# Scores behind the next pair's in-projection, and dense products beside the last gate table, in a trunk of token mixing and product-key experts

## The chip, the cores and the metric

The kernel runs on one core of a Trainium2 chip. The core's engines are TensorE (PE; its weight load is listed apart as PEld), VectorE (DVE), ScalarE (ACT), GpSimd (POOL) and SyncE (SP, which only issues transfers here). Each works off its own instructions in order, and waits where an operand is not there. What counts is the device time of one execution in microseconds (us), lower is better.

## The reference

One layer over 1024 rows (tokens) of 1024 columns, float32. A token mixer splits an in-projection into a gated convolution, a short convolution and a spatial gating, and projects back. Then comes the part that sets the time, a mixture of 16384 experts of one neuron each, 128 of which are picked for each token:

```python
q = (nf @ w_q).reshape(t, PEER_HEADS, D_KEY)                # 8 heads, two halves of 128
s1 = jnp.einsum("thd,hkd->thk", q1, sub_keys[:, 0])
s2 = jnp.einsum("thd,hkd->thk", q2, sub_keys[:, 1])
v1, i1 = lax.top_k(s1, TOPK)                                # 16 of 128 keys a half
v2, i2 = lax.top_k(s2, TOPK)
cand = (v1[..., :, None] + v2[..., None, :]).reshape(t, PEER_HEADS, TOPK * TOPK)
vals, ci = lax.top_k(cand, TOPK)                            # 16 of the 256 sums
idx = (e1 * N_KEYS + e2).reshape(t, PEER_HEADS * TOPK)
gates = jax.nn.softmax(vals, axis=-1)
# for each token t and each of its 128 picks k:
act = gelu(einsum("td,tkd->tk", xb, expert_u[idx])) * gates
out = einsum("tk,tkd->td", act, expert_v[idx])
```

A per-layer embedding with two projections and a final norm follow (the back).

## The kernel before

The rows are cut into eight tiles of 128. The kernel has three stages.

**Front.** Four pairs of tiles, (0,1), (2,3), (4,5), (6,7), go one after the other through `mix_in` (in-projection z, L158 and L207, in chunks through the PSUM tile `z`; convolution on VectorE, L179; norms; spatial gating, L232), `mix_out` (out-projection, L267, whose results are added to h, L269; normed h, L275, and its transposes) and `choose` (query product with w_q, L299; scores, L306; the top 16 of each half, L329 to L334; `select`, L338 to L394, which makes the keys, the gates and the indices). `mix_out` and `choose` call `fill()` sixteen times in a pair, and each call takes three steps from the list `filler`.

**Gate tables.** Four tiles (DENSE: 1 to 4) and one more (MIXED: 0) get a table of gates, expert block by token, built by `gate_table`. For four tokens at a time VectorE makes a one-hot of the first key (oh1, L415), and the one-hot of the second, times the gate, is made on POOL (L421) in every other group, else on ScalarE (L426, L427), or for MIXED on VectorE (L423). Four products (L430) put them together in a PSUM tile `gt`, ScalarE copies it to st (L431), and SyncE writes st to memory, Wd (L434). One product is recorded as two matmuls. The table of tile t is started once the tile's choose() is done; that of MIXED comes last, after its own activations are known: `u_step(MIXED, b, True)` gathers for it 128 rows of expert_u (POOL issues, L536; VectorE multiplies and sums up, L538, with three buffers `gathF`), and `u_step(GATHER[0], 0, True)` 32 more for tile 5.

**Dense and gathers.** For the four DENSE tiles all experts are computed. `u_stage(b)` does 24 matmuls for one block of 128 experts (L481 to L483, three for each of eight slices of columns, since a float32 factor is split into a high and a low part: uh by ScalarE, L468, ul by POOL, L470), then a gelu, the multiplication with the table w (L486) and the split into ah and al (L488, L490). `v_stage(g)` takes four blocks: ten products of twelve matmuls (L504 to L506) into the PSUM tile `mm` (two buffers), each of which VectorE adds to accA (L508). The fifth of the products' five tiles is MIXED, whose activations are its table itself (wm, split into mh and ml). `v` is split into vh and vl (L475 on ScalarE, L477 on POOL). Beside all this, `experts` gathers the experts of the three GATHER tiles (5 to 7): each of 128 gathers of u (L536, L538) and 128 of v (L566, L568) a tile is an issue on POOL and a product on VectorE, with five buffers.

**Back.** For each tile a norm, transposes (L594) and two projections (L612).

The order of the instructions on each engine isn't that of the text: the framework places them when the kernel is built, by its own simulated timeline, with the order of the text as priority, and the engines then keep that order. A pool of tiles that is laid where an earlier pool lay waits for the earlier pool's users; `fctx.close()` ends the pools of the front (work, gathF, group, wstream, rowp, wbp and the PSUM pool), and the pools of the dense stage come behind it.

## Time and profile before

| | us |
|---|---|
| median of three runs | 2855.62 |
| lowest and highest | 2852.89, 2864.11 |
| the profiled execution | 2862.61 |
| its span, first to last instruction | 2860.8 |
| TensorE busy | 2620.5 |
| VectorE busy | 2156.9 |
| POOL busy | 1945.5 |
| ScalarE busy | 1007.6 |

The profile is of one execution. A busy time is the time in which an engine worked on at least one instruction; what is left of the span is idle, and the trace names for each idle stretch the instruction whose end released it. "PEclk" is the clock that TensorE was granted, as a share of 2.4 GHz. In a window's row, the numbers behind the engines' busy times are counts of instructions.

### The profile page before, as it was taken

Reading aid. Unit: us, or ns where it says so; the run is one execution under the profiler, and the core shown is the slowest. Engines: PE = TensorE matmul, PEld = TensorE weight load, DVE = VectorE, ACT = ScalarE, POOL = GpSimd, SP = SyncE. Lnnn points to the kernel's source line nnn. Section 1 sums busy time; section 2 is a strip of 40 time slices with the busy share of each in tenths; the row PEclk is TensorE's granted clock in tenths of the full one; section 3 lists DMA queues with packets and bytes.
Section 4 is the critical chain, followed back from the end, with each engine's and each line's share of the span. In section 5 each row is a group of like instructions: output and inputs, shape, how many; then the busy total and the mean of one; then the engine's idle time right before and its main releaser. Section 6 shows DMA issues by size and latency. Waiting matters only on the chain.

```text
span 2860.8 us, 37645 instructions
## 1 busy us (share of the span) xinstructions
PE 2620.5 (92%) x12671; PEld 2203.2 (77%) x12671; DVE 2156.9 (75%) x4738; ACT 1007.6 (35%) x1930; POOL 1945.5 (68%) x1740
## 2 busy tenths in 40 slices
PE   7998999889678678999999999999999999999988
PEld 6887888688677656888787888878787788788767
DVE  5567888999977886777777777777777777677776
ACT  3312455335764544222322223232222322222342
POOL 0000377347876787888878888888887878888773
PEclk9998999899789779999999999999999999999999
DMA  6353688787657649899999999999999999999885
GB/s 203 129 185 120 236 300 301 242 304 253 221 206 274 228 184 339 317 324 344 331 333 328 331 347 330 338 329 342 325 336 329 328 348 332 335 339 324 299 290 174
DMA packets 299698, 820.92 MB, mean 287 GB/s; under 512 B 26096, under 2 KB 117616, under 8 KB 296944
## 3 DMA queue, kind: packets, MB, share of 16 engines
q0 software_dynamic: 129024, 469.82, 45.8%
q1 hardware_dynamic: 170480, 348.70, 35.6%
q8 instruction: 100, 1.64, 0.2%
q14 instruction: 94, 0.77, 0.1%
HBM read 764.93 MB, written 53.48 MB: 286 GB/s over the span
## 4 chain that ended last, share of the span: by engine, by line
PE 33%; DMA 23%; DVE 17%; POOL 13%; issue 10%; ACT 2%; SPq 0%; POOLq 0%; DVEq 0%; ACTq 0%
DMA g<-expert_u,idx 10%; DMA g<-expert_v,idx 10%; PE z L158 4%; DVE g L538 4%; POOL g L536 4%; PE mm L612 3%; POOL vl L477 3%; PE mm L504 3%; PE z L481 3%; PE z L482 3%; PE mm L505 3%; PE mm L506 3%; PE z L483 3%; PE mm L299 2%; PE mm L267 2%
## 5 line engine op out<-in xcount | busy, mean ns | idle before, releaser
L536 POOL DMA_INDIRECT g<-expert_u,idx x512 | 511.9, 1000 | 369.6 <-DVE g L538 163.2
L568 DVE SCALAR_TENSOR_TENSOR accP<-g,act,accP 128x1024 f32<-128x1024 f32 x384 | 493.2, 1284 | 210.9 <-DMA g<-expert_v,idx 207.4
L538 DVE SCALAR_TENSOR_TENSOR g<-g,nP 128x1024 f32<-128x1024 f32 x352 | 422.8, 1215 | 178.5 <-DMA g<-expert_u,idx 177.1
L566 POOL DMA_INDIRECT g<-expert_v,idx x384 | 367.7, 957 | 144.4 <-DVE accP L568 60.7
L504 PE MATMUL mm<-vh,ah 128*128 128x512 f32 x1024 | 400.3, 392 | 13.5 <-DVE accA L508 6.8
L481 PE MATMUL z<-nh,uh 128*128 128x512 f32 x1024 | 401.8, 393 | 8.1 <-DVE al L490 5.9
L482 PE MATMUL z<-nl,uh 128*128 128x512 f32 x1024 | 400.6, 391 | 2.0 <-DVE nl L446 2.0
L483 PE MATMUL z<-nh,ul 128*128 128x512 f32 x1024 | 400.2, 391 | 0.0
L505 PE MATMUL mm<-vl,ah 128*128 128x512 f32 x1024 | 399.2, 391 | 0.0
L506 PE MATMUL mm<-vh,al 128*128 128x512 f32 x1024 | 396.7, 390 | 0.0
L421 POOL TENSOR_SCALAR oh<-iota,eT,gT 128x128 f32<-128x128 f32 x320 | 314.5, 991 | 63.9 <-PE gt L430 50.8
L468 ACT CAST uh<-u 128x1024 fp32r<-128x1024 f32 x128 | 134.8, 1053 | 574.8 <-PE z L482 459.3
L477 POOL TENSOR_TENSOR vl<-v,vh 128x512 fp32r<-128x512 f32 x256 | 328.2, 1302 | 3.2 <-ACT vh L475 0.7
L470 POOL TENSOR_TENSOR ul<-u,uh 128x1024 fp32r<-128x1024 f32 x128 | 309.3, 2417 | 6.9 <-ACT uh L468 4.6
L430 PE MATMUL gt<-oh,oh 128*128 128x128 f32 x1280 | 221.4, 321 | 95.1 <-POOL oh L421 40.4
L430 PEld LDWEIGHTS gt<-oh,oh 128*128 128x128 f32 x1280 | 194.5, 224 | 123.1 <-POOL oh L421 82.6
L475 ACT CAST vh<-v 128x512 fp32r<-128x512 f32 x256 | 153.1, 621 | 306.9 <-DMA v<-expert_v 250.6
L538 DVE SCALAR_TENSOR_TENSOR g<-g,hrow 128x1024 f32<-128x1024 f32 x160 | 197.3, 1236 | 72.3 <-DMA g<-expert_u,idx 72.2
L158 PE MATMUL z<-aT,w 128*128 128x256 f32 x960 | 227.0, 393 | 16.0 <-DMA w<-w_inF 13.1
L299 PE MATMUL mm<-nT,w 128*128 128x256 f32 x1024 | 237.0, 383 | 4.4 <-DMA w<-w_q 4.4
L508 DVE TENSOR_TENSOR accA<-mm,accA 128x512 f32<-128x512 f32 x320 | 217.8, 684 | 27.0 <-PE mm L506 26.7
L504 PEld LDWEIGHTS mm<-vh,ah 128*128 128x128 f32 x1024 | 193.0, 189 | 56.7 <-DVE accA L508 9.8
(368 smaller groups left out, 4586.6 us busy)
## 6 DMA issues: line engine op xcount, KB each, us to landing
u<-expert_uT SPq DMA_DIRECT2D x128, 512.0 KB, 6.4
v<-expert_v SPq DMA_DIRECT2D x128, 512.0 KB, 4.9
Wd<-st SPq DMA_DIRECT2D x20, 2048.0 KB, 8.4
w<-w_q SPq DMA_DIRECT2D x64, 512.0 KB, 4.8
w<-Wd SPq DMA_DIRECT2D x128, 256.0 KB, 9.7
w<-w_inF SPq DMA_DIRECT2D x60, 512.0 KB, 3.6
wo<-w_out SPq DMA_DIRECT2D x32, 512.0 KB, 4.5
g<-expert_u,idx POOLq DMA_INDIRECT x512, 6.3
```

Source lines behind the costliest of these rows:

```text
L430: nc.tensor.matmul(pw[:, :, k], oh2[:, k], oh1[:, k], start=True, stop=True)
L477: nc.gpsimd.tensor_tensor(vl, v[:, s * 512:s * 512 + 512], vh.bitcast(F32), op=OP.subtract)
L481: nc.tensor.matmul(ph, uh[:, c], nh[:, c], start=c == 0, stop=False)
L482: nc.tensor.matmul(ph, uh[:, c], nl[:, c], start=False, stop=False)
L483: nc.tensor.matmul(ph, ul[:, c], nh[:, c], start=False, stop=c == 7)
L504: nc.tensor.matmul(po, ah[:, c], vh, start=i == 0, stop=False)
L505: nc.tensor.matmul(po, ah[:, c], vl, start=False, stop=False)
L506: nc.tensor.matmul(po, al[:, c], vh, start=False, stop=i == NG - 1)
L536: nc.gpsimd.indirect_dma_start(out=ug, out_offset=None, in_=expert_u, in_offset=bass.IndirectOffsetOnAxis(ap=idx[:, k:k + 1], axis=0))
L538: nc.vector.scalar_tensor_tensor(ug, ug, 1.0, ns[t, front], op0=OP.mult, op1=OP.mult, accum_out=dots[:, k - b * KB:k - b * KB + 1])
L566: nc.gpsimd.indirect_dma_start(out=vg, out_offset=None, in_=expert_v, in_offset=bass.IndirectOffsetOnAxis(ap=idx[:, kk:kk + 1], axis=0))
L568: nc.vector.scalar_tensor_tensor(acc, vg, act[:, k:k + 1], acc, op0=OP.mult, op1=OP.add)
```

## The change

Three things are changed.

The scores of a pair are computed one pair later. The loop now runs mix_in of a pair, then `finish` of the pair before (its choose, the list of tables to make, and for the last pair the gathers of MIXED), then mix_out of the pair. The last pair's `finish` stands behind the loop. (The branch `if t0 < 0` is never taken.)

Pools are laid out in another order. In the front, work and gathF stand behind group, wstream and rowp; wbp is allocated from the other side of the memory (`side="right"`); the tables' PSUM tiles (three of `gt`, and iotaP) have a pool of their own, psumT. Behind the front, psum2 is opened ahead of psumG, and hold and dm are allocated from the right.

The load of MIXED's wm and its split, and the loads of accA, stand in v_stage instead of u_stage and ahead of dense().

```diff
     fctx = ExitStack()
-    work = fctx.enter_context(tc.tile_pool(name="work", bufs=2))
-    gath = fctx.enter_context(tc.tile_pool(name="gathF", bufs=FG))
     group = fctx.enter_context(tc.tile_pool(name="group", bufs=1))
     wstream = fctx.enter_context(tc.tile_pool(name="wstream", bufs=2))
     rowp = fctx.enter_context(tc.tile_pool(name="rowp", bufs=2))
+    gath = fctx.enter_context(tc.tile_pool(name="gathF", bufs=FG))
+    work = fctx.enter_context(tc.tile_pool(name="work", bufs=2))
     fconst = fctx.enter_context(tc.tile_pool(name="fconst", bufs=1))
-    wbp = fctx.enter_context(tc.tile_pool(name="wbp", bufs=2))
+    wbp = fctx.enter_context(tc.tile_pool(name="wbp", bufs=2, side="right"))
     psum = fctx.enter_context(tc.tile_pool(name="psum", bufs=2, space=bass.MemoryType.PSUM))
+    psumT = fctx.enter_context(tc.tile_pool(name="psumT", bufs=3, space=bass.MemoryType.PSUM))
...
-    iotaP = psum.tile([P, P], F32, name="iotaP", bufs=1)
+    iotaP = psumT.tile([P, P], F32, name="iotaP", bufs=1)
...
-        pe = psum.tile([P, 4, P], F32, name="gt", bufs=3)
+        pe = psumT.tile([P, 4, P], F32, name="gt")
...
-                pw = psum.tile([P, P, 4], F32, name="gt", bufs=3)
+                pw = psumT.tile([P, P, 4], F32, name="gt")
...
                 ws[b // NG] = w
-                wm = dm.tile([P, P // TG, NG, TG], F32, name="wm")
-                nc.sync.dma_start(wm, Wd[MIXED][:, :, b:b + NG])
-                wm = wm.rearrange("p g n t -> p n g t")
-                mh = dm.tile([P, NG, P], F32R, name="mh")
-                mh_ = mh.rearrange("p n (g t) -> p n g t", t=TG)
-                nc.scalar.copy(mh_, wm)
-                ml = dm.tile([P, NG, P], F32R, name="ml")
-                nc.gpsimd.tensor_tensor(ml.rearrange("p n (g t) -> p n g t", t=TG), wm, mh_.bitcast(F32),
-                                        op=OP.subtract)
-                ms[b // NG] = mh, ml
...
         def v_stage(g):
+            b = g * NG
+            if g == 0:
+                for i, t in enumerate(TABLE):
+                    nc.sync.dma_start(accA[:, i], h1d[t])
+            wm = dm.tile([P, P // TG, NG, TG], F32, name="wm")
+            nc.sync.dma_start(wm, Wd[MIXED][:, :, b:b + NG])
+            wm = wm.rearrange("p g n t -> p n g t")
+            mh = dm.tile([P, NG, P], F32R, name="mh")
+            mh_ = mh.rearrange("p n (g t) -> p n g t", t=TG)
+            nc.scalar.copy(mh_, wm)
+            ml = dm.tile([P, NG, P], F32R, name="ml")
+            nc.gpsimd.tensor_tensor(ml.rearrange("p n (g t) -> p n g t", t=TG), wm, mh_.bitcast(F32),
+                                    op=OP.subtract)
+            ms[b // NG] = mh, ml
...
-    for t0, nt in ((0, 2), (2, 2), (4, 2), (6, 2)):
-        yT = mix_in(t0, nt)
-        choose(t0, nt, mix_out(t0, nt, yT))
+    def finish(t0, nt, nT):
+        choose(t0, nt, nT)
         if t0 == UAT:
             for b in range(P // KB):
                 u_step(MIXED, b, True)
         filler.extend(gate_table(t0 + t) for t in range(nt) if t0 + t in DENSE)
         if t0 == GAT:
             filler.append(gate_table(MIXED))
+
+    waits = []
+    for t0, nt in ((0, 2), (2, 2), (4, 2), (6, 2)):
+        yT = mix_in(t0, nt)
+        while waits:
+            finish(*waits.pop())
+        waits.append((t0, nt, mix_out(t0, nt, yT)))
+        if t0 < 0:
+            finish(*waits.pop())
+    finish(*waits.pop())
...
     fctx.close()
+    psum = ctx.enter_context(tc.tile_pool(name="psum2", bufs=2, space=bass.MemoryType.PSUM, reuse_waits="tile"))
     psumG = ctx.enter_context(tc.tile_pool(name="psumG", bufs=1, space=bass.MemoryType.PSUM, reuse_waits="tile"))
-    psum = ctx.enter_context(tc.tile_pool(name="psum2", bufs=2, space=bass.MemoryType.PSUM, reuse_waits="tile"))
-    hold = ctx.enter_context(tc.tile_pool(name="hold", bufs=1, reuse_waits="tile"))
+    hold = ctx.enter_context(tc.tile_pool(name="hold", bufs=1, side="right", reuse_waits="tile"))
     gath = ctx.enter_context(tc.tile_pool(name="gath", bufs=BG, reuse_waits="tile"))
     accA = hold.tile([P, NT, D], F32, name="accA")
-    for i, t in enumerate(TABLE):
-        nc.sync.dma_start(accA[:, i], h1d[t])
...
-    dm = dctx.enter_context(tc.tile_pool(name="dm", bufs=2, reuse_waits="tile"))
+    dm = dctx.enter_context(tc.tile_pool(name="dm", bufs=2, side="right", reuse_waits="tile"))
```

Where the instructions stand is seen by engine. In the changed kernel's rows, a line of the table's part is one higher than before (L431 for L430), and a line of u_stage nine lower (L472 for L481).

TensorE at the end of the MIXED table, before. L430 are table products of two groups (oh with their numbers), L481 to L483 those of u_stage:

```order
L430 MATMUL gt<-oh_8494,oh_8496 128x128
L430 MATMUL gt<-oh_8507,oh_8509 128x128
L430 MATMUL gt<-oh_8494,oh_8496 128x128
L430 MATMUL gt<-oh_8507,oh_8509 128x128 x3
L430 MATMUL gt<-oh_8494,oh_8496 128x128 x2
L481 MATMUL z<-nh,uh 128x512 x2
L482 MATMUL z<-nl,uh 128x512
L483 MATMUL z<-nh,ul 128x512
```

All 128 table products stand ahead of the first u-product. TensorE in the changed kernel, behind the first 58 table products:

```order
L431 MATMUL gt<-oh_8285,oh_8287 128x128
L472 MATMUL z<-nh,uh 128x512 x2
L431 MATMUL gt<-oh_8298,oh_8300 128x128
L431 MATMUL gt<-oh_8285,oh_8287 128x128
L431 MATMUL gt<-oh_8298,oh_8300 128x128 x3
L431 MATMUL gt<-oh_8285,oh_8287 128x128
L473 MATMUL z<-nl,uh 128x512
L474 MATMUL z<-nh,ul 128x512
```

The first u-products stand among the table's. TensorE in the changed kernel, at the end of the table, where L509 to L511 are the v-products:

```order
L431 MATMUL gt<-oh_8510,oh_8512 128x128
L472 MATMUL z<-nh,uh 128x512
L473 MATMUL z<-nl,uh 128x512
L474 MATMUL z<-nh,ul 128x512
L509 MATMUL mm<-vh,ah 128x512 x2
L510 MATMUL mm<-vl,ah 128x512
L511 MATMUL mm<-vh,al 128x512
```

165 u-products now stand ahead of the last table product, three more behind it, and then all 120 v-products of the first group in a row.

POOL at the end of the MIXED table, before. L421 are the table's one-hots, L536 gather issues of u, L470 ul, L462 ml, L477 vl:

```order
L421 TENSOR_SCALAR oh_8496<-iota,eT,gT 128x128 x4
L536 DMA g<-expert_u,idx 128x1024 x7
L470 TENSOR_TENSOR ul<-u,uh 128x1024
L536 DMA g<-expert_u,idx 128x1024
L470 TENSOR_TENSOR ul<-u,uh 128x1024
L462 TENSOR_TENSOR ml<-wm,mh 128x512
L477 TENSOR_TENSOR vl<-v,vh 128x512 x2
L536 DMA g<-expert_u,idx 128x1024
L477 TENSOR_TENSOR vl<-v,vh 128x512 x2
```

POOL there, in the changed kernel (L422, L541, L461, L496 and L468 are the same five):

```order
L461 TENSOR_TENSOR ul<-u,uh 128x1024
L422 TENSOR_SCALAR oh_8499<-iota,eT,gT 128x128 x4
L461 TENSOR_TENSOR ul<-u,uh 128x1024 x2
L541 DMA g<-expert_u,idx 128x1024 x7
L468 TENSOR_TENSOR vl<-v,vh 128x512 x4
L541 DMA g<-expert_u,idx 128x1024 x3
L496 TENSOR_TENSOR ml<-wm,mh 128x512 x2
L541 DMA g<-expert_u,idx 128x1024 x2
L468 TENSOR_TENSOR vl<-v,vh 128x512 x4
L541 DMA g<-expert_u,idx 128x1024 x5
```

Seven of the ul subtractions stand among the one-hots and two more ahead of the gather issues, and the fifteenth gather issue behind the table now stands behind two ml and eight vl. VectorE at the first addition into accA, before, where L538 are gather products, L486 the multiplication with the table, L490 the split and L508 the addition:

```order
L486 TENSOR_TENSOR z<-z,w 128x512
L538 SCALAR_TENSOR_TENSOR g,dots<-g,nP 128x1024
L490 TENSOR_TENSOR al<-z,ah 128x512
L486 TENSOR_TENSOR z<-z,w 128x512
L538 SCALAR_TENSOR_TENSOR g,dots<-g,nP 128x1024
L490 TENSOR_TENSOR al<-z,ah 128x512
L538 SCALAR_TENSOR_TENSOR g,dots<-g,nP 128x1024 x2
L486 TENSOR_TENSOR z<-z,w 128x512
L538 SCALAR_TENSOR_TENSOR g,dots<-g,nP 128x1024
L490 TENSOR_TENSOR al<-z,ah 128x512
L538 SCALAR_TENSOR_TENSOR g,dots<-g,nP 128x1024
L508 TENSOR_TENSOR accA<-mm,accA 128x512
```

VectorE there, in the changed kernel (L543, L477 and L513 are the gather product, the multiplication and the addition, L416 and L424 the table's one-hots):

```order
L416 TENSOR_TENSOR oh_8497<-iotaP,eT 128x512
L416 TENSOR_TENSOR oh_8510<-iotaP,eT 128x512
L424 TENSOR_SCALAR oh_8512<-iotaP,eT,gT 128x128 x4
L477 TENSOR_TENSOR z<-z,w 128x512 x2
L536 TENSOR_TENSOR nP<-nP,g_ffn 128x1024
L543 SCALAR_TENSOR_TENSOR g,dots<-g,nP 128x1024 x15
L513 TENSOR_TENSOR accA<-mm,accA 128x512 x2
L543 SCALAR_TENSOR_TENSOR g,dots<-g,nP 128x1024 x2
```

Before, 18 gather products stand ahead of the first addition, with multiplications and splits between them; now 15 stand in a row between the last multiplication of the table's time and the first addition.

## Rows read from the trace of the kernel before

**Rows 1.** The page's head, parts 1 and 2: busy time of the engines, granted clock by slice.

```profile
PE 2620.5 (92%) x12671; PEld 2203.2 (77%) x12671; DVE 2156.9 (75%) x4738; ACT 1007.6 (35%) x1930; POOL 1945.5 (68%) x1740
...
PEclk9998999899789779999999999999999999999999
```

**Rows 2.** Windows, all engines; columns as in their first line.

```profile
core 0: us, PE busy (x) PEld busy (x) DVE busy (x) ACT busy (x) POOL busy (x), PEclk, DMA share, GB/s
...
290.00:773.00 483.00, 418.53 (x2471) 371.60 (x2470) 436.53 (x1447) 228.72 (x523) 284.07 (x262) 0.93 0.76 267
773.00:1018.40 245.40, 190.47 (x1096) 172.47 (x1095) 196.89 (x753) 151.75 (x364) 178.51 (x173) 0.81 0.62 222
1018.40:1055.00 36.60, 23.64 (x113) 20.14 (x112) 27.44 (x73) 11.66 (x19) 28.94 (x34) 0.73 0.64 247
1055.00:1084.40 29.40, 23.24 (x147) 18.80 (x146) 22.88 (x54) 10.51 (x19) 27.50 (x36) 0.97 0.57 221
1084.40:1130.00 45.60, 34.91 (x128) 26.98 (x129) 30.21 (x49) 22.10 (x34) 31.36 (x25) 0.85 0.97 351
1130.00:1250.00 120.00, 120.00 (x530) 99.09 (x529) 84.83 (x108) 33.61 (x52) 97.07 (x82) 1.00 0.93 329
```

**Rows 3.** VectorE's waits from 290 to 1018 us: total, times, longest.

```profile
DVE g L538 <- DMA g<-expert_u,idx: 72.2, 39, 5.6
```

**Rows 4.** Window around the start of pair 1's out-projection; columns as in rows 2.

```profile
257.00:290.00 33.00, 20.98 (x93) 14.65 (x93) 29.87 (x182) 17.46 (x36) 0.56 (x1) 0.72 0.24 79
```

**Rows 5.** The page, parts 5 and 6: count, busy us, mean ns; us to landing.

```profile
L477 POOL TENSOR_TENSOR vl<-v,vh 128x512 fp32r<-128x512 f32 x256 | 328.2, 1302 | 3.2 <-ACT vh L475 0.7
L470 POOL TENSOR_TENSOR ul<-u,uh 128x1024 fp32r<-128x1024 f32 x128 | 309.3, 2417 | 6.9 <-ACT uh L468 4.6
...
L538 DVE SCALAR_TENSOR_TENSOR g<-g,hrow 128x1024 f32<-128x1024 f32 x160 | 197.3, 1236 | 72.3 <-DMA g<-expert_u,idx 72.2
...
g<-expert_u,idx POOLq DMA_INDIRECT x512, 6.3
```

**Rows 6.** TensorE's timeline around 782 us: start, length, line, count.

```profile
781.94 1.95 PE L430 MATMUL gt<-oh,oh 128*128 128x128 f32 x16
783.73 0.94 PE L267 MATMUL mm<-wo,yT 128*128 128x128 f32 x7
```

**Rows 7.** TensorE's timeline, end of the MIXED table and start of the dense stage.

```profile
1079.11 2.04 PE L430 MATMUL gt<-oh,oh 128*128 128x128 f32 x14 [0.28 <-DVE oh L423]
1081.48 0.49 PE L430 MATMUL gt<-oh,oh 128*128 128x128 f32 x2 [0.33 <-POOL oh L421]
1082.34 1.95 PE L430 MATMUL gt<-oh,oh 128*128 128x128 f32 x14 [0.37 <-DVE oh L423]
1086.52 0.73 PE L481 MATMUL z<-nh,uh 128*128 128x512 f32 x2 [2.23 <-ACT nh L445]
...
1088.86 0.63 PE L481 MATMUL z<-nh,uh 128*128 128x512 f32 x1
1089.29 0.63 PE L482 MATMUL z<-nl,uh 128*128 128x512 f32 x1
...
1109.63 1.22 PE L504 MATMUL mm<-vh,ah 128*128 128x512 f32 x2 [6.55 <-ACT vh L475]
```

**Rows 8.** POOL's timeline, the same stretch.

```profile
1058.37 25.38 POOL L421 TENSOR_SCALAR oh<-iota,eT,gT 128x128 f32<-128x128 f32 x32 [0.75 <-PE gt L430]
...
1091.13 0.94 POOL L536 DMA_INDIRECT g<-expert_u,idx  x1 [0.30 <-issue]
1092.37 0.94 POOL L536 DMA_INDIRECT g<-expert_u,idx  x1 [0.30 <-issue]
...
1109.75 1.29 POOL L462 TENSOR_TENSOR ml<-wm,mh 128x512 fp32r<-128x512 f32 x1
```

**Rows 9.** VectorE's timeline, its first addition into accA.

```profile
1139.00 0.69 DVE L508 TENSOR_TENSOR accA<-mm,accA 128x512 f32<-128x512 f32 x1 [3.07 <-PE mm L506]
```

**Rows 10.** Timelines of VectorE and TensorE: last gather product, last tile's transposes.

```profile
2828.86 1.28 DVE L568 SCALAR_TENSOR_TENSOR accP<-g,act,accP 128x1024 f32<-128x1024 f32 x1
...
2836.08 1.03 PE L594 MATMUL z<-ident,a 128*128 128x128 f32 x8
```

## The prediction

> **What bounds the kernel now.** I read the page's head first: TensorE is busy for 2620.5 us of the span, 92% [rows 1], so on average little is left to win, and the line of granted clocks falls under nine tenths only within the first 15 of the 40 slices. Then I cut the span by stage. The reader is to compare the busy time of each engine with the length of its stretch [rows 2]. From 1130 us on TensorE is busy throughout (120.00 of 120) at the full clock. Before that three stretches differ. From 290 to 1018.4 us, the front with the last three pairs, VectorE is busy for 436.53 of 483.00 and 196.89 of 245.40 us, 95 us short of all, and the list of its waits puts 72.2 us of those on gathers that had not landed [rows 3]. So the front is nearer to a VectorE bound than to a TensorE bound (418.53 and 190.47). From 1018.4 to 1084.4 us the mixed tile's table is made, and TensorE idles for 13.0 and 6.2 us. From 1084.4 to 1130 us the dense stage starts, and TensorE idles for another 10.7 us.
>
> The start of the dense stage can be given as a line. 128 matmuls were recorded up to 1130 us and 530 more in the next 120 us, one each 0.2264 us. Carried back, 658 x 0.2264 = 149 us before 1250, so at full pace the stage would have begun at 1101.0 us: 46.0 us behind 1055 us, the time by which 58 of the table's 128 products are done. I call 1055 us the midpoint, since the changed order puts the first dense product behind the same 58. Everything after is a line of dense products, so what the change is worth in the middle is how far this line moves, measured from the midpoint.
>
> **Part 1: choose() behind the next pair's in-projection.** No work is added or removed. Where a pair's out-projection starts, TensorE waits for the convolution's end on VectorE and ScalarE: around pair 1 it is busy for 20.98 of 33 us, at a clock of 0.72 [rows 4], and there are three such places. They are what deferring the scores fills. But VectorE is busy for 29.87 of those 33 us, and in the new order its own work is the same; filling TensorE there moves its work forward, and VectorE, which also has the top-16 searches and 160 gather products to do, ends when it ended. The gathers start later too, since the mixed tile's indices come out of the first choose(): 37 instead of 62 gather products stand ahead of the third pair's residual adds, 102 instead of 119 ahead of the fourth's, 158 instead of 160 ahead of the mixed table's first one-hot. The lead that TensorE gains is therefore paid back by the table. Bounds: at best VectorE loses every idle time but the gather waits, 95 - 72.2 = 23 us; at worst the 25 gather products that fall behind come out serial, at 1.24 us each [rows 5] 31 us later. I take -1, nearest to the counts at the table, which are within 2 of each other.
>
> **Part 2: dense products beside the mixed table.** The pools and banks are laid out anew so that the dense stage's buffers don't wait for the front's. In the order, the first u-product stands behind 58 table products, and 165 u-products stand before the last table product. TensorE's part of the second half: 70 table products at 0.224 us (16 records, two to a product, between the starts at 781.94 and 783.73 [rows 6]) are 15.7 us, and 165 x 0.2264 = 37.4 us, together 53 us. The table alone took 29.4 us there, paced by the one-hots on POOL and VectorE, 3.2 us to 8 products (16 records between the starts at 1079.11 and 1082.34 [rows 7]). POOL now also has 7 ul passes to do in it: 28.5 us for 36 one-hots at 0.79 (25.38 us for 32 [rows 8]) and 7 x 2.417 [rows 5] are 45 us, so TensorE stays the longest. I allow up to 9 us for in-order waits or for 48 products at the lower clock, where two products start 0.43 us apart rather than 0.2264 [rows 7]: 53 to 62, of which I take 55.
>
> What comes next is the part that I count against the change. Before, the dense products began 2.23 us behind the table [rows 7], the first v-product at 1109.63, and VectorE's first add into accA at 1139.00, behind 18 gather products that stood between small pieces of dense work [rows 9]. Now VectorE has 15 gather products in a row ahead of that first add, and no piece of dense work in between; the two PSUM buffers of the v-products fill with 24 matmuls, and the next one waits for the add. The 15 products wait for POOL, which has between the last one-hot and the 15th gather: 2 ul (4.8 us), 15 issues at the pitch of 1.24 us (18.6), 8 vl at 1.302 (10.4) and 2 ml at 1.29 (2.6), in all 36.4 us, from the starts 1091.13 and 1092.37 and the means [rows 5, 8]. Then the gather lands (6.3 us), is multiplied (1.2) and the add ends (0.7): 44.6 us behind POOL's last one-hot. POOL may be up to 5 us ahead of TensorE, so the third v-product starts 40 to 45 us behind the last table product. By then TensorE has done 165 + 3 u-products and 24 v-products, 192, worth 43.5 us of the line.
>
> Line after, from the midpoint: 53 + 40 - 43.5 = 49.5 at the least, 62 + 45 - 43.5 = 63.5 at the most, 55 + 44 - 43.5 = 55.5 taken. Before it was 46.0. So the dense stage is +3.5 to +17.5 us, I take +10. The table overlaps indeed, but the products that were put forward are the ones that waited for nothing before, and the first accumulation still waits for gathers that couldn't be issued during the table.
>
> **Part 3: wm and accA loaded in v_stage.** Per group of four expert blocks one SyncE load, one ScalarE cast and one POOL subtraction move from the u-stage to before the v-products, and the five loads of accA move into the first group; on SyncE they then stand behind the first loads of v. The count is the same, and the adds into accA wait for the gathers anyway. Nothing, as long as that 40 us wait is there; gone, it would cost one load ahead of the first add, for which the nearest row is a gather's 6.3 us [rows 5].
>
> **Tail.** 51 instead of 46 gathers are left after the last add into accA. The last gather product ends at 2828.86 + 1.28 and TensorE is busy with the back until 2836.08, when the last tile's transposes start [rows 10]: about 6 us of slack. Five gathers at 1.24 us each are 6.2 us, at 8.8 us for a ring of five (issue, landing, product) 8.8 us: 0 to +3, I take +1.5.
>
> **Sum.** -1 + 10 + 0 + 1.5 = +10.5 us. The profiled execution took 2862.61 us, 1.75 us over its span and 0.24% above the median of the runs, 2855.62; it becomes 2873, and the median 2866, +0.37%.
>
> **The rivals.** *Lockstep, slower.* In-order engines may not overlap the two streams at all. VectorE's w-multiplies stand between one-hots, so that a late u-product holds the table's next one-hot, and a late one-hot holds the u-products queued behind its table product. Then the second half is the sum of both, 29.4 + 37.4 = 66.8, and with gaps that hold the clock down for 48 products of the 165, 9.6 more: 76. The line moves to 76 + 43 - 43.5 = 75.5, +29.5, 2885 or 2886 with the tail. For it: TensorE's rows in the table are runs of 14 and 2 with a wait for an engine ahead of each [rows 7]. Against it: POOL and VectorE have room. It decides from a second half above 61 us, where the sum passes 0.5%.
>
> *The front gains, faster.* If the three bubbles at the out-projections are closed and VectorE's idle time that is not a gather wait goes with them, the front is 23 us shorter, and without the middle's loss 2833; with a part of it about 2840. For it: the low clock of 0.72 there, that the added work would lift. Against it: VectorE at 90%.
>
> *It does what it says, faster.* The table costs nothing, since dense products fill TensorE's idle time in all three stretches, 13.0 + 6.2 + 10.7 = 29.9 us, and the gathers land in time: 2826. For it: the idle time is there. Against it: the 15 gather products in a row. The Trainium skill, page "Perfetto Trace Analysis", section "Optimization Strategy", says that a kernel with several regimes may gain from interleaving them; by that rule, this is the result. The trace agrees in so far as the table and the dense stage have different busiest engines; no run here shows the two interleaved.
>
> **How the numbers follow.** The forecast has 0.45 with a range of its own of 2857 to 2879; lockstep 0.28; the front 0.15; the full overlap 0.12. About 0.5%, 14.3 us, is what a measurement of this kernel can tell from no change. The forecast's range passes 2870 with a ninth of its chance, 0.05. So: slower 0.28 + 0.05 = 0.33, the same 0.40, faster 0.15 + 0.12 = 0.27. The range for 8 in 10 runs from 2831, just below the front's case, to 2890, above lockstep; the full overlap and a still worse table are left out.
>
> **What would show it.** In the profile after: the table's last product 53 to 62 us behind its 59th; one TensorE wait of some 25 us or more for accA's add before the third v-product, with VectorE waiting for gathers from expert_u; a line 50 to 63 us from the midpoint; the midpoint itself within some 5 us of 1055. A midpoint earlier by 15 us or more shows the front's case; a TensorE without that one wait shows the full overlap; a second half above 66 us lockstep. I am wrong if the gathers are issued early enough, by a POOL that runs ahead of the table, to land before the table ends.

## The result, and the profile after

The changed kernel is slower. Its median is 2879.85 us, that of the kernel before, run beside it, 2855.95 us (11 runs each); the ratio is 1.0078, with a 95% interval of 1.0061 to 1.0096, so the change costs about 22 us, more than the 0.5% that can be told from none. The forecast was 2866 us, +10.5 us, which is within that 0.5%.

The traces show a part of this. The profiled execution took 2875.26 us (span 2873.5), 12.7 us more than that of before; a second pair of executions, e9 and e10 below, differs by 13.0 us. The two of before lie 6.7 and 11.8 us above the median of before, those of after 4.6 us below and 0.9 us above theirs. So the traces can account for about 13 us of the 22, and where the other 9 are is in no trace.

The page's head of the kernel after, parts 1 and 2, against [rows 1]:

```profile
PE 2606.5 (91%) x12671; PEld 2192.3 (76%) x12671; DVE 2160.6 (75%) x4738; ACT 1005.7 (35%) x1930; POOL 1962.5 (68%) x1740
...
PEclk9999999899889677999999999999999999999999
DMA  6354587777657667999999999999999999999885
```

TensorE and ScalarE work a little less than before, VectorE 3.7 and POOL 17.0 us more, and both of these have idle time left. The windows of after, with the columns of [rows 2]:

```profile
1018.40:1055.00 36.60, 23.63 (x118) 19.71 (x118) 35.03 (x88) 18.03 (x28) 32.27 (x28) 0.76 0.64 207
1055.00:1084.40 29.40, 26.58 (x151) 23.04 (x151) 18.55 (x39) 12.08 (x20) 24.84 (x24) 1.00 0.29 110
1084.40:1130.00 45.60, 27.09 (x145) 22.60 (x145) 23.41 (x44) 15.55 (x24) 27.72 (x26) 0.83 0.78 282
1130.00:1250.00 120.00, 104.98 (x441) 84.95 (x440) 79.84 (x108) 28.88 (x46) 94.46 (x83) 0.89 0.95 336
```

From 1055 to 1084.4 us TensorE is now busy for 26.58 of 29.40 us, against 23.24. In the next two stretches it gives this back: 27.09 instead of 34.91 of 45.6, and 104.98 instead of 120.00 of 120. The next column to look at is the last but one, the share of time in which the DMA engines moved something: 0.29 and 0.78, where it was 0.57 and 0.97.

The milestones, each worked out from the trace of one execution (us from the span's start; the midpoint is the start of the 59th of the mixed table's 128 products; the line is worked out as in the prediction, at 0.2267 us a product, from the count up to 1250 and up to 2640 us):

| | before | before again | after | after again |
|---|---|---|---|---|
| last score product | 964.1 | 971.4 | 946.0 | 949.2 |
| midpoint | 1056.8 | 1065.4 | 1052.2 | 1054.5 |
| the mixed table's last product ends | 1084.3 | 1092.9 | 1109.0 | 1111.3 |
| line of dense products, to 1250 | 1101.3 | 1109.7 | 1111.5 | 1114.0 |
| line of dense products, to 2640 | 1142.0 | 1148.3 | 1149.0 | 1153.5 |
| last add into accA starts | 2727.5 | 2730.9 | 2729.2 | 2734.9 |
| last gather product starts | 2828.9 | 2834.1 | 2841.1 | 2846.6 |
| span | 2860.8 | 2866.0 | 2873.5 | 2879.0 |

The second half of the table takes 56.8 us in both executions instead of 27.5. The delay of the dense products shrinks on the way: 10.2 and 4.3 us in the line up to 1250 us, 1.7 and 4.0 us at the last add into accA. The last gather product is 12.3 and 12.5 us later, nearly as much as the span. TensorE's timeline at its start and its end, of after:

```profile
1051.03 0.49 PE L431 MATMUL gt<-oh,oh 128*128 128x128 f32 x2 [0.73 <-POOL oh L422]
1051.27 0.73 PE L472 MATMUL z<-nh,uh 128*128 128x512 f32 x2
1051.87 1.58 PE L431 MATMUL gt<-oh,oh 128*128 128x128 f32 x12
...
1107.28 1.72 PE L431 MATMUL gt<-oh,oh 128*128 128x128 f32 x14
1122.76 1.22 PE L509 MATMUL mm<-vh,ah 128*128 128x512 f32 x2 [13.06 <-ACT vh L466]
1129.42 0.80 PE L510 MATMUL mm<-vl,ah 128*128 128x512 f32 x1 [5.45 <-POOL vl L468]
...
1147.45 1.22 PE L509 MATMUL mm<-vh,ah 128*128 128x512 f32 x2 [13.39 <-ACT vh L466]
```

u-products (L472) and table products (L431) do run side by side. Then TensorE waits three times, for 13.06, 5.45 and 13.39 us, and each time for the split of v. The wait that the prediction had named, for VectorE's first add into accA, isn't there. VectorE's timeline, first of before, then of after, shows its first gather product for the gather tiles and (after) its first add:

```profile
1088.31 1.21 DVE L538 SCALAR_TENSOR_TENSOR g<-g,nP 128x1024 f32<-128x1024 f32 x1
```

```profile
1113.65 1.22 DVE L543 SCALAR_TENSOR_TENSOR g<-g,nP 128x1024 f32<-128x1024 f32 x1
...
1154.17 1.49 DVE L513 TENSOR_TENSOR accA<-mm,accA 128x512 f32<-128x512 f32 x2 [9.26 <-POOL vl L468]
```

The add comes 45 us behind the table's last product, as forecast (44.6), but VectorE stood idle ahead of it for 9.26 us: it waited for TensorE's product (the row names vl, an operand of that product), and not TensorE for it. The first gather product stands 4.7 us behind the end of the table, much as before (4.0); it is 25.3 us later because the table ends 24.7 us later. Where the v's are late is seen on SyncE's queue and on ScalarE, of after:

```profile
1109.91 0.33 SPq L435 DMA_DIRECT2D Wd<-st  x1
...
1114.04 1.68 SPq L463 DMA_DIRECT2D v<-expert_v  x2
1117.41 2.24 SPq L488 DMA_DIRECT2D accA<-h1d  x5
1119.95 4.16 SPq L490 DMA_DIRECT2D wm<-Wd  x2
1124.69 8.79 SPq L533 DMA_DIRECT2D hrow<-h1d  x1
1133.58 2.85 SPq L463 DMA_DIRECT2D v<-expert_v  x2
```

```profile
1122.09 1.14 ACT L466 CAST vh<-v 128x512 fp32r<-128x512 f32 x2 [2.34 <-DMA v<-expert_v]
...
1143.42 0.62 ACT L494 CAST mh<-wm 128x512 fp32r<-128x512 f32 x1 [17.64 <-DMA wm<-Wd]
...
1146.78 1.14 ACT L466 CAST vh<-v 128x512 fp32r<-128x512 f32 x2 [1.94 <-DMA v<-expert_v]
```

The first two v's are asked for only behind the last write of the table, the next two 19.5 us later. POOL gives the first buffer back at 1130.60 us, and SyncE is held by the issue of hrow until 1133.48 us. Between the two pairs stand the five loads of accA and two of wm, whose cast holds ScalarE for 17.64 us. But the next vh, behind that cast, waits another 1.94 us for its own v, which lands 13.2 us after it was asked for. So what comes last is v and not the cast. The transfers issued from 1085 to 1165 us, with KB and median us to landing:

```profile
v<-expert_v SPq DMA_DIRECT2D x7, 512.0 KB, 8.0
...
accA<-h1d SPq DMA_DIRECT2D x5, 512.0 KB, 14.2
...
wm<-Wd SPq DMA_DIRECT2D x4, 256.0 KB, 12.8
```

Before, the first two v's also left 8 us behind the table's last write, and the next two 20 us later (1084.94, 1093.04 and 1113.54 us on SyncE). But then TensorE had all its u-products of the first group still to do, which covered them.

The end of the trace, ScalarE before, then ScalarE and TensorE after, against [rows 10]:

```profile
2833.31 1.15 ACT L588 ACTIVATE a<-hrow,r 128x1024 f32<-128x1024 f32 x1 [0.94 <-POOL r L122]
```

```profile
2846.05 1.13 ACT L593 ACTIVATE a<-hrow,r 128x1024 f32<-128x1024 f32 x1
2847.24 1.09 PE L599 MATMUL z<-ident,a 128*128 128x128 f32 x8 [3.80 <-ACT a L593]
```

Before, TensorE was through with the tile ahead at 2836.2 us and found the last tile's normed rows ready since 2834.5. After, it comes at 2843.4, 7.2 us later, and then waits another 3.80 us for them, since the last gather product is 12.3 us later. With 1.5 us of half-clock products behind this wait (30 products in 8.60 instead of 7.11 us) that is 12.5 of the 12.7 us. So in these traces it is the gathers that carry the loss to the end.

### The profile page after: what moved, and what is told of

Its sections match the earlier page's. It is cut to its first block, busy times and chain, and to the rows that moved or that the text cites. A ratio compares the mean times of both kernels' runs of the same rounds, so it can differ in the third digit from the quotient of the medians.

```text
span 2873.5 us, 37623 instructions
## 1 busy us (share of the span) xinstructions
PE 2606.5 (91%) x12671; PEld 2192.3 (76%) x12671; DVE 2160.6 (75%) x4738; ACT 1005.7 (35%) x1930; POOL 1962.5 (68%) x1740
## 3 DMA queue, kind: packets, MB, share of 16 engines
q0 software_dynamic: 129024, 469.82, 45.6%
## 4 chain that ended last, share of the span: by engine, by line
PE 40%; DMA 19%; DVE 19%; POOL 12%; issue 9%; ACT 1%; SPq 0%; POOLq 0%; DVEq 0%; ACTq 0%
DMA g<-expert_u,idx 9%; DMA g<-expert_v,idx 7%; DVE g L543 5%; PE mm L509 5%; PE z L472 4%; PE mm L510 4%; PE mm L511 4%; PE z L473 4%; PE z L474 4%; PE z L159 4%; PE mm L617 3%; POOL oh L422 3%; POOL g L541 3%; POOL vl L468 3%; PE mm L300 2%
## 5 line engine op out<-in xcount | busy, mean ns | idle before, releaser
L541 POOL DMA_INDIRECT g<-expert_u,idx x512 | 512.7, 1001 | 307.3 <-DVE g L543 130.3
L543 DVE SCALAR_TENSOR_TENSOR g<-g,nP 128x1024 f32<-128x1024 f32 x352 | 424.0, 1216 | 222.4 <-DMA g<-expert_u,idx 220.1
L509 PE MATMUL mm<-vh,ah 128*128 128x512 f32 x1024 | 403.3, 395 | 35.7 <-ACT vh L466 26.5
L472 PE MATMUL z<-nh,uh 128*128 128x512 f32 x1024 | 401.1, 392 | 9.6 <-DVE al L481 9.6
L511 PE MATMUL mm<-vh,al 128*128 128x512 f32 x1024 | 399.2, 393 | 1.0 <-DVE al L481 1.0
L422 POOL TENSOR_SCALAR oh<-iota,eT,gT 128x128 f32<-128x128 f32 x320 | 330.3, 1041 | 45.9 <-PE gt L431 40.9
L431 PE MATMUL gt<-oh,oh 128*128 128x128 f32 x1280 | 222.5, 321 | 127.8 <-DVE oh L416 66.6
L468 POOL TENSOR_TENSOR vl<-v,vh 128x512 fp32r<-128x512 f32 x256 | 328.1, 1301 | 3.4 <-ACT vh L466 0.9
L431 PEld LDWEIGHTS gt<-oh,oh 128*128 128x128 f32 x1280 | 198.2, 226 | 154.8 <-POOL oh L422 96.5
L461 POOL TENSOR_TENSOR ul<-u,uh 128x1024 fp32r<-128x1024 f32 x128 | 309.8, 2421 | 8.1 <-ACT uh L459 6.1
L543 DVE SCALAR_TENSOR_TENSOR g<-g,hrow 128x1024 f32<-128x1024 f32 x160 | 196.4, 1229 | 81.7 <-DMA g<-expert_u,idx 81.6
L509 PEld LDWEIGHTS mm<-vh,ah 128*128 128x128 f32 x1024 | 194.2, 190 | 82.0 <-ACT vh L466 27.6
L513 DVE TENSOR_TENSOR accA<-mm,accA 128x512 f32<-128x512 f32 x320 | 218.2, 684 | 30.7 <-PE mm L511 21.1
```

Source lines behind the costliest of these rows:

```text
L422: nc.gpsimd.tensor_scalar(oh2[:, k], iota, k2, gk, op0=OP.is_equal, op1=OP.mult)
L431: nc.tensor.matmul(pw[:, :, k], oh2[:, k], oh1[:, k], start=True, stop=True)
L468: nc.gpsimd.tensor_tensor(vl, v[:, s * 512:s * 512 + 512], vh.bitcast(F32), op=OP.subtract)
L472: nc.tensor.matmul(ph, uh[:, c], nh[:, c], start=c == 0, stop=False)
L509: nc.tensor.matmul(po, ah[:, c], vh, start=i == 0, stop=False)
L511: nc.tensor.matmul(po, al[:, c], vh, start=False, stop=i == NG - 1)
```

## The experiments

Where nothing else is said, ratios are to runs of the kernel before on the same chip.

### Part 1 alone, and parts 2 and 3 alone

The kernel before with the new loop (e1):

```diff
+    def finish(t0, nt, nT):
+        choose(t0, nt, nT)
...
     for t0, nt in ((0, 2), (2, 2), (4, 2), (6, 2)):
         yT = mix_in(t0, nt)
-        choose(t0, nt, mix_out(t0, nt, yT))
+        while waits:
+            finish(*waits.pop())
+        waits.append((t0, nt, mix_out(t0, nt, yT)))
+    finish(*waits.pop())
```

> The kernel before with part 1 alone: the scores of a pair behind the next pair's in-projection, pools and banks as before. The line from which the dense products run at full pace stood at 1101.3 us before and at 1111.5 us in the changed kernel. If the loss lies at the start of the dense stage (both theories below), the dense products start behind the table as before, the line stays within 4 us of 1101 and the time within 0.3% of the kernel before. If the delayed scores cost by themselves (fewer gathers done in the front, more of them left over behind the dense stage), the time is 0.4 to 0.8% above the kernel before with the dense line unmoved.

The kernel after with the old order of the scores (e2):

```diff
-        if t0 < 0:
+        if t0 >= 0:
             finish(*waits.pop())
-    finish(*waits.pop())
```

> The changed kernel with part 1 undone: each pair's scores follow its out-projection at once; pools, banks and the loads in v_stage as changed. If the loss lies at the start of the dense stage, it stays: 0.4 to 0.9% above the kernel before, with TensorE waiting for 25 us or more in pieces behind the table. If it is the delayed scores that cost, the time comes back to within 0.3% of the kernel before.

Measured: e1 2856.27 us, 0.9996 (0.998 to 1.0011); e2 2867.65 us, 1.0029 (1.0013 to 1.0044). e1's time is that of the kernel before, but its line isn't within 4 us of 1101: it stands at 1091.5, with the midpoint 18.5 us earlier than in before, in an execution that is the shortest of its twelve. e2's 0.29% is under the 0.4 to 0.9% of the one case and just inside the 0.3% of the other. The two parts together cost 0.78%, so parts 2 and 3 cost more where the scores are late. Why is not shown; in e2 the first u-product stands behind 17 of the 128 table products instead of 58, so that more of the table is there to be covered. TensorE's waits for v are there in e2 as well, from 1085 to 1200 us two for vh of 20.1 us in sum.

### A third buffer for v

```diff
-            v = dv.tile([P, D], F32, name="v")
+            v = dv.tile([P, D], F32, name="v", bufs=3)
```

> The changed kernel with three buffers for v instead of two, nothing else. Theory A (15 gather products of VectorE ahead of the first addition into accA hold the third v-product): 12 instead of 15 stand ahead of it now, so the line from which the dense products run at full pace moves from 1111.5 by 4 to 7 us at most, and TensorE's wait before the third block stays on the addition. Theory B (the loads behind the table come late: v of the third block waits for a buffer that POOL frees only behind seven gather issues, and TensorE waited 13.4 us for its cast): that wait falls under 6 us, and the line moves by 7 to 13 us, to 1099 to 1105; the time falls by 0.2 to 0.5% against the changed kernel.

Measured: 2884.44 us, 1.0082 (1.0061 to 1.0104). The line of products starts 0.9 us behind the table's last product instead of 2.5, and the two waits for vh are 26.7 us in sum, as in after (26.5). The third v is now loaded with the first two and its cast starts at 1121.43 us, so the second wait has moved from the third block to the fourth, whose v leaves at 1129.39 us only. Its buffer was free at 1124.29 us, but SyncE was held by the issue of hrow until 1129.29 us. A missing buffer alone isn't what makes the later v's late.

### Without the loads of accA

The kernel after; the five tiles' residual h is left out of the result, since the first group of products is copied into accA instead of added to what was loaded:

```diff
-            if g == 0:
-                for i, t in enumerate(TABLE):
-                    nc.sync.dma_start(accA[:, i], h1d[t])
...
-                nc.vector.tensor_add(o_, po, o_)
+                if g == 0:
+                    nc.vector.tensor_copy(o_, po)
+                else:
+                    nc.vector.tensor_add(o_, po, o_)
```

> The changed kernel without the five loads of accA (2.5 MB) behind the table; the first group's additions are copies, so the residual h1 of the five tiles is left out of what is computed. Theory A: 14 instead of 15 gather products ahead of the first write of accA, the line moves by 1 to 2 us. Theory B, with the traffic of the loads as its cause: 2.5 MB at the 400 GB/s of that stretch are 6 us, by which wm and v land earlier, and the line moves by 4 to 8 us.

Measured: 2870.99 us, 1.0049 (1.0032 to 1.0066). TensorE's timeline at the same two v-products:

```profile
1116.27 1.22 PE L506 MATMUL mm<-vh,ah 128*128 128x512 f32 x2 [13.34 <-ACT vh L466]
...
1130.68 1.22 PE L506 MATMUL mm<-vh,ah 128*128 128x512 f32 x2 [3.77 <-ACT vh L466]
```

The first wait stays, the second falls from 13.39 to 3.77 us, and the line starts 5.0 us ahead of the table's last product instead of 2.5 behind it: 7.5 us. SyncE's issue of hrow takes 0.33 instead of 8.79 us, and the next v leaves at 1123.48 us, as soon as POOL has freed its buffer. The ratios differ by 0.29%, 8 us, though their intervals just overlap. So 2.6 MB of accA loads (five of 512 KB) in front of wm and of the next v's cost some 8 us, about a third of the loss.

### The first loads of v during the table

The kernel after with v in a pool of its own, laid where the table doesn't hold it:

```diff
-            v = dv.tile([P, D], F32, name="v")
+            v = dvv.tile([P, D], F32, name="v")
...
+    dvv = dctx.enter_context(tc.tile_pool(name="dvv", bufs=2, reuse_waits="tile"))
     da = dctx.enter_context(tc.tile_pool(name="da", bufs=5, reuse_waits="tile"))
```

> The changed kernel with the two buffers of v in a pool of their own that is laid ahead of da, over memory that the front frees earlier; the order then has the first two loads of v among the table's products instead of behind the last table write. Theory B1 (late v holds the first v-product): TensorE's wait of 13.1 us ahead of the first v-product falls to 8 us or less and the line from which the dense products run at full pace, which stood 2.5 us behind the last table product, stands 3 to 10 us ahead of it. Theory B2 (the burst of accA's 2.5 MB holds wm and the third block's v): the first wait goes, but a like wait appears at the third block, and the line moves by less than 3 us. Theory C (the gather stream of POOL and VectorE, which starts only when the table ends, sets the end): the time falls by less than half of what the line moves.

Measured: 2879.26 us, 1.0057 (1.0038 to 1.0077). The line starts 2.2 us ahead of the table's last product, 4.7 us better than in after. The first wait for vh falls from 13.06 to 3.24 us, the second is 16.63 us. ScalarE's timeline ahead of it:

```profile
1152.32 0.62 ACT L494 CAST mh<-wm 128x512 fp32r<-128x512 f32 x1 [18.71 <-DMA wm<-Wd]
...
1155.69 1.14 ACT L466 CAST vh<-v 128x512 fp32r<-128x512 f32 x2 [1.95 <-DMA v<-expert_v]
```

It is the wait of after again: wm and the next v's come behind the accA loads. The buffer of the next v is free at 1135.20 us, the v leaves at 1143.73 and lands at 1155.67. In time, e5 can't be told from after: the two intervals overlap widely.

### Gather products beside the table

Three kernels shift what can run beside the table by the PSUM banks, two of them by these alone. In e6 the u-products' tile z and the normed rows nP of the gathers lie over the front's banks, the v-products' mm and accP over the table's; e7 is e6 with the v pool of e5; in e8 psumG is opened ahead of psum2, as before the change.

```diff
-            ph = psum.tile([P, T], F32, name="z")
+            ph = psumZ.tile([P, T], F32, name="z")
...
-            n = h if front else psumG.tile([P, D], F32, name="nP")
+            n = h if front else psumN.tile([P, D], F32, name="nP")
...
+    psumZ = ctx.enter_context(tc.tile_pool(name="psumZ", bufs=2, space=bass.MemoryType.PSUM, reuse_waits="tile"))
+    psumN = ctx.enter_context(tc.tile_pool(name="psumN", bufs=1, space=bass.MemoryType.PSUM, reuse_waits="tile"))
```

> The changed kernel with another order of PSUM banks: z and nP (the normed row that gather products read) lie over the front's banks and mm and accP over the table's, so that gathers of the dense stage can be multiplied while the table is made. In the order 32 more gather products and 7 issues of expert_v stand ahead of the table's second half, and 48 u-products instead of 165 ahead of its last product. Theory C (8 gathers fewer done at 1200 us put the last gather product 12 us later, and that sets the end): gathers done at 1200 us rise from 194 to 215 or more, the last gather product falls to 2800 to 2825 us, and the time falls to within 0.3% of the kernel before or below it, although fewer dense products run beside the table. Theory B (the dense line alone): the line moves to later, and the time stays at or above that of the changed kernel.

> Both edits: PSUM banks in the other order, and v in a pool of its own. If the two causes add up, the time is that of the run with the banks alone less what the early v gave by itself, 0.1 to 0.4%; if only the gather stream counts, it is that of the run with the banks alone.

```diff
-    psum = ctx.enter_context(tc.tile_pool(name="psum2", bufs=2, space=bass.MemoryType.PSUM, reuse_waits="tile"))
     psumG = ctx.enter_context(tc.tile_pool(name="psumG", bufs=1, space=bass.MemoryType.PSUM, reuse_waits="tile"))
+    psum = ctx.enter_context(tc.tile_pool(name="psum2", bufs=2, space=bass.MemoryType.PSUM, reuse_waits="tile"))
```

> The changed kernel with one line put back: nP and accP lie over the front's PSUM banks and z and mm over the table's, as before. No dense product can stand beside the table then; instead some 50 gathers of the dense stage stand beside it, and the scores stay delayed. If the gather stream sets the end (theory C), the time falls to the kernel before or below it. If the dense line sets it (theory D), what counts is when the table ends and how soon 10 accumulations can follow: the gathers lengthen the table on POOL and VectorE, the line stands 1125 us or later, and the time is 0.7 to 1.5% above the kernel before although the last gather product comes 20 us or more earlier than in the changed kernel.

Measured: e6 2897.85 us, 1.0125 (1.0109 to 1.014); e7 2888.31 us, 1.0099 (1.0083 to 1.0114); e8 2916.68 us, 1.0205 (1.0182 to 1.0227), more than expected. In e6 and e7 the last gather product starts at 2818.7 and 2806.9 us, 22 and 34 us earlier than in after, but the line starts at 1142.3 and 1133.0, 31 and 22 us later. In e8 the last gather product starts at 2784.7 us, 56 us earlier than in after, and the kernel is the slowest of all. Its windows show why:

```profile
1055.00:1084.40 29.40, 17.31 (x76) 14.46 (x74) 29.40 (x63) 7.19 (x12) 26.62 (x29) 0.62 0.72 256
1084.40:1130.00 45.60, 30.88 (x126) 24.58 (x125) 44.38 (x86) 12.20 (x19) 41.29 (x46) 0.65 0.70 253
```

VectorE is busy for 29.40 of 29.40 and 44.38 of 45.60 us: the gather products take it from the one-hots, TensorE waits for the table at a clock of 0.62 and 0.65, the table's last product comes at 1125.2, and the line starts at 1159.5. So gathers that come early don't help if the dense products come late.

### The kernels after, before and e1, a second time

> A second profiled execution of the changed kernel. The line, counted from the last table product, within 2 us of the first one (2.5 us behind it), and 8 to 10 gathers fewer at 1200 us than before; what differs between the two executions lies ahead of the table.

> A second profiled execution of the kernel before. The line 16 to 18 us behind the last table product, as in the first one (17.0); the midpoint of the table may differ by up to 10 us, which is the part of the spread of the times that lies in the front.

> A second profiled execution of the kernel with the delayed scores alone, whose first one was the fastest of its twelve. If the delayed scores save time in the front, the last score product is again some 20 us earlier than before (940.2 against 964.1); the time, taken from twelve executions to be that of the kernel before, says that the lead is given back by the end of the table, so its midpoint should be within 8 us of the second execution of before.

Measured, one execution each: 2880.79, 2867.8 and 2852.59 us. What lies behind the midpoint came again: the line 2.7 us behind the table's last product (2.5), 16.8 us in before (17.0), 17.7 us in e1 (17.6); TensorE's waits for vh 26.5 us in sum, the longest 13.4; 193 gather products done by 1200 us instead of 199 (first pair 194 and 203), 6 fewer where 8 to 10 were expected. What lies between traces scatters: the midpoint of before moved by 8.6 us. In e1 the last score product came 21.8 us earlier than in the second execution of before, as expected, but the midpoint 17.7 us earlier and not within 8: the lead wasn't given back by the table. The spans of the two executions of e1 are 15.3 and 15.4 us below those of before, while the medians differ by no more than the noise, so a difference of two spans alone, up to some 15 us, decides nothing here.

### Nothing but loads and splits beside the table

> The kernel after with the PSUM tiles of the dense stage dealt out so that neither the u-products (z) nor the table tiles' gather products (nP) can begin before the mixed table's last product: both lie over the table's banks, while the v-products' tile mm and accP lie over the front's. The delayed scores, the pools on the other side and the loads in v_stage stay; v has a pool of its own, so that its first loads go out during the table. So the table runs beside loads and splits of u and the normed h alone.
>
> Theory D (the dense line sets the end, and whatever is put beside the table lengthens it by about what it saves): the 70 last table products take 28 to 38 us again instead of 57 to 59; the line of dense products starts 5 to 15 us behind the table's last product (17 in the kernel before); gathers done by 1200 us 193 to 203; ratio to the kernel before 0.995 to 1.002.
>
> Rival E (the loss is the burst of loads and gather issues behind the table, whatever ran beside it): the line starts 17 us or more behind the last table product, with two TensorE waits of over 10 us for vh, and the ratio stays at 1.003 or more.
>
> Rival F (the table is held by the splits of u and the loads of the dense stage, not by its products): the 70 table products take over 45 us although no dense product stands among them, and the ratio is 1.005 or more.

```diff
+    psumN = ctx.enter_context(tc.tile_pool(name="psumN", bufs=1, space=bass.MemoryType.PSUM, reuse_waits="tile"))
+    psumZ = ctx.enter_context(tc.tile_pool(name="psumZ", bufs=2, space=bass.MemoryType.PSUM, reuse_waits="tile"))
...
+    dvv = dctx.enter_context(tc.tile_pool(name="dvv", bufs=2, reuse_waits="tile"))
```

(with z, nP and v allocated from these pools, as in e6 and e5). Measured: 2874.44 against 2862.57 us, 1.0053 (1.0037 to 1.0069). The 70 table products take 33.7 us, the line starts 8.7 us behind the last, at 1089.3, and 200 gather products are done by 1200 us, as theory D expected of each; the ratio is not within its bounds. Rival E's ratio is met without its mechanism, since in the trace no wait for vh is left, and rival F's table isn't there. The profiled execution is the shortest of its 12, with the span of before, 2860.8 us, although its line of dense products is 12 us earlier. TensorE, and VectorE, at its end:

```profile
2833.68 1.97 PE L599 MATMUL z<-ident,a 128*128 128x128 f32 x8 [11.40 <-ACT a L593]
```

```profile
2826.70 2.61 DVE L573 SCALAR_TENSOR_TENSOR accP<-g,act,accP 128x1024 f32<-128x1024 f32 x2
```

TensorE waits 11.40 us for the last tile, whose last gather product starts at 2828.0, as in before (2828.9). The dense products were made to start early, the gathers weren't, and the gain is spent in this wait. Why the other eleven executions are longer is in no trace.

## Why the prediction was right or wrong

**The number.** The measured median, 2879.85 us, lies within the range of 2831 to 2890 and just above the forecast's own 2857 to 2879. That the sum of +10.5 us is near the 12.7 and 13.0 us of the traces is in part luck: the wait that it rests on wasn't there, the line's delay had shrunk to 1.7 and 4.0 us by the last add, and the 12.3 us of the gathers were put at 1.5.

**Two streams set the end.** In all traces the span stands in one of two relations (counted from the start of the last product and of the last add):

| | end behind last gather product | end behind last add into accA |
|---|---|---|
| before, again | 31.9, 31.9 | 133.3, 135.1 |
| e1, again | 32.0, 31.9 | 135.7, 137.1 |
| after, again | 32.4, 32.4 | 144.3, 144.1 |
| e2, e3 | 32.2, 31.5 | 140.8, 141.0 |
| e4, e5, e12 | 34.0, 34.3, 32.8 | 143.9, 149.7, 149.5 |
| e6, e7, e8 | 84.2, 75.7, 130.2 | 133.8, 134.3, 128.4 |

Either the gathers end some 32 us ahead of the end, or the adds into accA some 128 to 135 us; in before both hold at once, and in after, e2 to e5 and e12 the gathers come last. The prediction put the bound on TensorE from 1130 us on. That is half of it: the kernel before is balanced between the dense products and the gathers, and the change delays both, the gathers for good, the dense products mostly for a time.

**Part 1: right in size, its mechanism not shown.** Taken at -1 us, measured alone at 0.9996. With everything in place the midpoint is 4.6 and 10.9 us earlier, within the bounds of -23 to +31. But that the table pays the lead back isn't what the traces of e1 show, where the midpoint is 18.5 and 17.7 us earlier; whether the lead is lost behind it or lies in the spread of the executions stays open.

**The table beside dense products: right.** The second half of the table was forecast at 55 us and takes 56.8; lockstep (above 61) didn't come. (58 products were done at 1056.8 us and not at 1055, so that before the second half took 27.5 us and the line stood 44.5 us from the midpoint, not 46.0.)

**The wait behind the table: right size by luck, wrong cause.** The line was forecast 55.5 us from the midpoint and is at 59.3 and 59.5, within the 49.5 to 63.5; against before it moved by 10.2 us in the first pair (forecast +10) and by 4.3 in the second. But the step that led there, TensorE waiting for an add held up by 15 gather products, failed: these products were done 9 us before the add could start. What stood in its place is three waits for the split of v, 31.9 us in sum. The part that holds is its last sentence: the u-products that were put forward had waited for nothing, and by waiting for nothing they had been the cover under which v and wm were loaded and split. What was overlooked is what else starts at the table's end: the two v's, and only 19.5 us later the next two. A third buffer (e3) moves the second gap by one block, an earlier first load (e5) closes the first only.

**Part 3: wrong, by some 8 us.** It was set at nothing as long as the add waits for gathers, with a gather's landing of 6.3 us as the nearest price otherwise. The wait wasn't there, and e4 gives the price of accA's loads in their new place. They land in 14.2 us at the median, more than twice the row taken. Before, they left during the table and landed in 10.3 us at the median, out of the way of v and wm:

```profile
1038.27 4.91 SPq L648 DMA_DIRECT2D accA<-h1d  x5
```

**The tail: the term that was mis-sized.** It was set at +1.5 us, from five more gathers behind the last add at 1.24 us each, less 6 us of slack. The count of five is near: the gathers are nine behind at 1200 us (194 done against 203) and five to seven from 2000 us on (875 against 882 by 2800 us), in the first pair. They start later because the table ends later, and nP lies over banks that the table holds; in e8, where the two PSUM pools alone change places, the first gather product comes at 956.8 us. Two things were wrong. The gathers' pace isn't that of the product alone: 524 of them from 1400 to 2640 us are 2.36 us each. And the slack was under 2 us: of the 6 us between the last gather product and the transposes, 4.3 are the copy, the squares and the norm of the last tile on ScalarE and POOL (done at 2834.5, transposes at 2836.1). Five gathers at 2.36 us are 11.8 us; measured are 12.3 us at the last gather product.

**The rivals.** The sign named for the full overlap, a TensorE without the wait for the add, was there, and misled: the waits for v stood in its place. The sign of the front's gain, a midpoint 15 us earlier, didn't come in after; it came in both traces of e1, and the median showed no gain. The Trainium skill, page "Perfetto Trace Analysis", section "Optimization Strategy", says that interleaving regimes with different busiest engines may improve performance. No kernel here agrees: u-products beside the table give 1.0078 and 1.0029 (after, e2), gather products beside it 1.0099 to 1.0205 (e6, e7, e8). The most contended engine does change between the regimes, but VectorE, POOL and the queues of SyncE and ScalarE, which feed both, are the same.

**What stays open.** 9 of the 22 us are in no trace. Nor is it settled why the gathers don't make up their delay while the dense products make up part of theirs. From 1250 to 2640 us the DMA engines move 334 GB/s at a share of 0.95 before and after, which suggests that the transfers pace both streams: by 1250 us 300.5 and 297.9 MB had been moved in the two executions of before, 295.9 and 295.0 in those of after, and 4.7 and 2.9 MB at 334 GB/s are 14 and 9 us, against 12.7 and 13.0 us of span. But the second pair fits less well, no kernel changed the bytes alone, and in e8 the most had been moved by then (306.5 MB) in the longest run, so this remains argued.

## What to carry to other kernels

Before work that waits for nothing is moved into an idle stretch, ask what it covered where it stood: here it was the loading and splitting of the next operands, which can't move along while their buffers and the queues are taken. Where two streams end together, a gain needs both: count the slower one's steps at its own pace, not at the length of one instruction, and measure slack from the last operand's readiness and not from the last big instruction. And loads put in front of a consumer's loads on one queue cost what they take to land in that crowd: 14.2 us here, against 10.3 where they stood before.

## What was not expected of the hardware

- In the burst behind the table the first two loads of wm (256 KB), issued behind accA's, land after 23.4 and 22.1 us, the next two after 3.5 and 3.4 (after). The median of the four, 12.8 us, describes none of them.
- Behind accA's five loads the issue of one load on SyncE's queue itself takes 7.8 to 8.8 us (hrow in after, e3 and e5); without them it takes 0.33 (e4).
- After a wait of 13 us TensorE's wide products follow each other at 0.43 us, at a granted clock of 0.50, the lower of its two levels, as those from 1130.02 to 1133.43 us in after; at the full level they take 0.2267 us. These waits are therefore paid for twice, the second time in the products behind them.
- Two executions of one kernel differ by 8.6 us ahead of the dense stage already (the midpoint of before at 1056.8 and 1065.4 us).
